# A decoder trunk on one core: fixing the order of VectorE and ScalarE from the second half of the output projection to the second classic pair

## The chip, the cores and the metric

The kernel runs on one core of one Trainium2 chip. The metric is the device time of one execution in microseconds (us); the time before is the median of three executions. In the profile PE is TensorE (matmuls), DVE is VectorE, ACT is ScalarE, POOL is GpSimd and SP is SyncE, which issues the DMAs. The program is one fixed list of instructions per engine; each engine works through its list in order and waits at an instruction whose inputs or buffers are not ready.

## What is computed

One layer with a sequence of 1024 tokens and a width of 1024, all in float32:

```python
h = _rmsnorm(x, norm1_g) * (1.0 + sc1) + sh1
z = h @ w_in
# forgetting attention on q, k, v and causal pooling on u give "mixed"
x = x + g1 * (mixed @ w_out)
h = _rmsnorm(x, norm2_g) * (1.0 + sc2) + sh2
a = h @ ffn_up                  # 1024 -> 2*2816
conv = conv_b + causal depthwise conv of width 3 of a
gate, val = split(conv, 2)
x = x + g2 * ((silu(gate) * val) @ ffn_down)
return _rmsnorm(x, final_g)
```

## The kernel before, in words

Every float32 product is made of three matmuls: an operand is split into a high part (a cast) and a low part (the operand minus its cast), and high by high, high by low and low by high are added in PSUM. So each operand of TensorE costs one cast, mostly on ACT, and one subtraction, mostly on DVE.

Around the change the work runs through these steps. Tokens come in eight tiles of 128 (t = 0 to 7).

- **Output projection, second half** (`wo_gen(1, t)`, then `wo_finish(1, t)`): TensorE fills the bank `po` of tile t; DVE multiplies by the gate (`ot`, L1129) and adds to the residual `x1[t]` (L1130); SP stores it (L1132). ACT squares and sums (L1135), ACT and DVE make the reciprocal root (L230, L231, L236 to L239, 128x1 each), DVE scales `xn` (L1137).
- **Transposition** (`make_h2T(t)`, called two steps later): TensorE transposes `xn` in eight 128x128 pieces (L1166), ACT evicts four of them (L1171) and DVE four (L1173) into `hn`, ACT casts the high part `HIb` (L1176), and the low part `LOb` is subtracted at L1178, on GpSimd for t below 6 and on DVE for t = 6 and 7. The transposes of tiles 6 and 7 stand inside the first classic banks.
- **Sums** (`tsums(t)`, t = 0 to 3): tiles t and t + 4 are combined on DVE (L1186, L1188, L1189, L1192) into three operands, and each is split (`put_quad`: ACT casts at L1153, DVE subtractions at L1155). They fill the `TQ` tiles 1, 2 and 3. Each TQ tile takes a quarter from each t, so it is whole after `tsums(3)`. `put_t4(t)` (L1197, L1198) puts the last of the sums back into `HIb` and `LOb`.
- **The MLP's up-projection.** Its columns come in 22 units of 128 gate and 128 value columns. Units 0 and 1 are "classic": four banks `uc` each (gate or value, first or second 512 tokens), 24 matmuls per bank (L1348 to L1350), copied out by ACT (L1353); `gate` and `value` then do the convolution (ACT L1361, DVE L1363 twice), Silu (ACT L1307, with a table load), the product (L1311) and its split. From unit 2 on a unit takes seven products of 12 matmuls (a Strassen scheme; banks `ua`, `ub`, `uc`) in the order 1, 5, 6, 2, 7, 3, 4. Product 1 reads `HIb` and `LOb`; product 5 reads TQ tile 1, product 6 TQ tile 2 and adds onto the bank of product 1, which ACT copies out first (L1323).
- **Weights of the units**: `load_x_up(j)` issues the loads of `wraw` on SP (L1238). `prep(j, p)` makes the left operand of a product: sums on DVE (L1268 to L1277) and a split by `hl` (ACT L1250, DVE L1251). From unit 2 on `wraw` lies in the same pool of nine buffers ("qk") as `x1` and `hn`, so a load waits until the last reader of an old `hn` is done.

TensorE's order is written out by hand for the whole program. For DVE and ACT a hand-written order (a `manual_schedule` block for the two engines in `ENG`) ends with the attention; from the output projection on the tile scheduler sets it, and it mixes the steps above.

Of the kernel before, what the change touches and what calls it, by code (L numbers as in the profile page):

```python
# [21 lines left out]
KT = D // 128  # L22
TT = S // 128
# [27 lines left out]
def kernel(  # L51
# [7 lines left out]
    nc = tc.nc  # L59
# [30 lines left out]
    def Tmx(name, shape=(128, 1024), dt=F32):  # L90
        return T("mx", list(shape), dt, name, 8)
# [885 lines left out]
    def wo_gen(dh, t):  # L977
        ts_ = slice(t * 128, (t + 1) * 128)
        po = pos[dh, t] = B1("po")
        for n, k in enumerate(KORD):  # L980
            while not (k in split_done and (dh, k) in wo):
                bg(1, 1, 1)
            h, l = wo[dh, k]
            mm(po, lhsT=HI[k][:, ts_], rhs=h, start=n == 0, stop=False)  # L984
            yield
            mm(po, lhsT=HI[k][:, ts_], rhs=l, start=False, stop=False)  # L986
            yield
            mm(po, lhsT=LO[k][:, ts_], rhs=h, start=False, stop=n == KT - 1)  # L988
            yield
# [130 lines left out]
    acth = dr.tile([NF, 128, S], F32, name="acth")  # L1120
    actl = dr.tile([NF, 128, S], F32, name="actl")

    def wo_finish(dh, t):
        ds_ = slice(dh * 512, (dh + 1) * 512)
        if dh == 0:
            x1.append(Tqk(f"x1{t}", (128, 1024), F32))
            nc.sync.dma_start(out=x1[t], in_=x[t * 128:(t + 1) * 128, :])
        tmp = Tpt("ot", (128, 512), F32)
        nc.vector.tensor_mul(out=tmp, in0=pos[dh, t], in1=g1b[:, ds_])  # L1129
        nc.vector.tensor_add(out=x1[t][:, ds_], in0=x1[t][:, ds_], in1=tmp)  # L1130
        if dh == 1:
            nc.sync.dma_start(out=x1d[t], in_=x1[t])  # L1132
            xn = Tp("xn")
            ss = Ts("ss2", 1)
            nc.scalar.activation(out=xn, in_=x1[t], func=AF.Square, accum_out=ss)  # L1135
            y = rstd_of(ss, "n2")
            nc.vector.tensor_scalar(out=xn, in0=x1[t], scalar1=y, scalar2=None, op0=ALU.mult)  # L1137
            hns[t] = xn

# [13 lines left out]
            nc.vector.tensor_sub(out=quad(n, 1, k)[:, :, cs], in0=s[:, 2 * k:2 * k + 2, :],  # L1155
                                 in1=f(quad(n, 0, k)[:, :, cs]))

    def make_h2T(t):
        ts_ = slice(t * 128, (t + 1) * 128)
        xn = hns[t]  # L1160
        hn = hn_[t] = Tqk("hn", (128, 1024), F32)
        for g in range(2):
            tp = B1("tp2")
            for q in range(4):
                j = g * 4 + q
                nc.tensor.transpose(tp[:, q * 128:(q + 1) * 128], xn[:, j * 128:(j + 1) * 128], ident)  # L1166
            for q in range(4):
                j = g * 4 + q
                o, i_ = hn[:, j * 128:(j + 1) * 128], tp[:, q * 128:(q + 1) * 128]
                if g == 0:  # L1170
                    nc.scalar.activation(out=o, in_=i_, func=AF.Identity, scale=A2[:, j:j + 1], bias=H2[:, j:j + 1])  # L1171
                else:
                    nc.vector.tensor_scalar(out=o, in0=i_, scalar1=A2[:, j:j + 1], scalar2=H2[:, j:j + 1],  # L1173
                                            op0=ALU.mult, op1=ALU.add)
        hv = hn.rearrange("p (a b) -> p a b", b=128)
        nc.scalar.copy(out=HIb[:, :, ts_], in_=hv)  # L1176
        eng = nc.gpsimd if t < 6 else nc.vector
        eng.tensor_sub(out=LOb[:, :, ts_], in0=hv, in1=f(HIb[:, :, ts_]))  # L1178

    def tsums(t):  # L1180

        cs = slice(t * 128, (t + 1) * 128)
        ha, hb = (hn_[a].rearrange("p (a b) -> p a b", b=128) for a in (t, t + 4))
        a1, a2, b1, b2 = ha[:, 0:4, :], ha[:, 4:8, :], hb[:, 0:4, :], hb[:, 4:8, :]
        V = nc.vector
        V.tensor_sub(out=a1, in0=b1, in1=a1)  # L1186
        put_quad(1, a1, cs)
        V.tensor_sub(out=b1, in0=b2, in1=b1)  # L1188
        V.tensor_sub(out=b2, in0=b2, in1=a1)  # L1189
        put_quad(2, b2, cs)  # L1190
        put_quad(3, b1, cs)
        V.tensor_sub(out=a2, in0=a2, in1=b2)  # L1192

    def put_t4(t):
        a2 = hn_[t].rearrange("p (a b) -> p a b", b=128)[:, 4:8, :]
        ts_ = slice(512 + t * 128, 640 + t * 128)
        nc.scalar.copy(out=HIb[:, 0:4, ts_], in_=a2)  # L1197
        nc.vector.tensor_sub(out=LOb[:, 0:4, ts_], in0=a2, in1=f(HIb[:, 0:4, ts_]))  # L1198

    for t in range(TT):  # L1200
# [4 lines left out]
    for t in range(TT):
        take(wo_gen(1, t), 99)
        wo_finish(1, t)
        if t >= 2:
            make_h2T(t - 2)

# [14 lines left out]
    def load_x_up(j):  # L1228
        for m in range(2):
            c0 = m * DFF + j * 128  # L1230
            if j == 0:
                hs = [Twr("wraw", (128, 4, 128)) if (m, k) != (1, 1) else
                      Tfb("wraw")[:, 0:512].rearrange("p (a b) -> p a b", b=128) for k in range(2)]
            else:
                r = (Tp if j == 1 else Tqk)("wraw", (128, 8, 128), F32)
                hs = [r[:, 0:4, :], r[:, 4:8, :]]
            for k in range(2):
                nc.sync.dma_start(out=hs[k], in_=ffn_up[k * 512:(k + 1) * 512, c0:c0 + 128]  # L1238
                                  .rearrange("(k p) c -> p k c", p=128))
                X[j, m, k] = hs[k]  # L1240
# [59 lines left out]
    def get(j, n, w=1024):  # L1300
        if (j, n) not in cpy:
            cpy[j, n] = (Tmx if j < NCL or n in ("p15", "u2") else Tqk)(n, (128, w), F32)
        return cpy[j, n]

    def gate(j):
        tg = cpy[j, "tg"] = conv(get(j, "cg"), j, "tg")
        nc.scalar.activation(out=tg, in_=tg, func=AF.Silu)  # L1307
# [31 lines left out]
    def classic(j, seq, after):

        done = {}
        for n, (m, ch) in enumerate(seq):
            b = B1("uc")
            sl = slice(ch * 512, (ch + 1) * 512)
            for k in range(KT):
                h, l = WT[j, (m, k // 4)]
                h, l = h[:, k % 4, :], l[:, k % 4, :]
                mm(b, lhsT=h, rhs=HI[k][:, sl], start=k == 0, stop=False)  # L1348
                mm(b, lhsT=h, rhs=LO[k][:, sl], start=False, stop=False)
                mm(b, lhsT=l, rhs=HI[k][:, sl], start=False, stop=k == KT - 1)  # L1350
                if j == 0 and (n, k) in ((0, 2), (1, 1)):
                    make_h2T(6 + n)
            nc.scalar.copy(out=get(j, "cv" if m else "cg")[:, sl], in_=b)  # L1353
            done[m] = done.get(m, 0) + 1
            if done[m] == 2:
                (value if m else gate)(j)
            after(n)
# [10 lines left out]
    for m in range(2):
        l2 = Tmx("ul0", (128, 8, 128), R)
        for k in range(2):  # L1370
            hl(0, (m, k), X[0, m, k], l2[:, 4 * k:4 * k + 4, :])
    load_x_up(1)
    for m in range(2):
        for k in range(2):
            hl(1, (m, k), X[1, m, k])

    def after0(n):
        if n:
            tsums(n - 1)

    def after1(n):
        if n == 0:
            tsums(3)
            load_x_up(2)
        if n == 1:
            for t in range(4):
                put_t4(t)

    classic(0, ((0, 0), (1, 0), (0, 1), (1, 1)), after0)
    classic(1, ((0, 1), (1, 1), (0, 0), (1, 0)), after1)  # L1390
# [239 lines left out]
```

## Time and profile before

| what | value |
|---|---|
| median of 3 executions | 1147.97 us (1146.52 to 1148.39) |
| the profiled execution: time, span | 1145.94 us, 1144.2 us |
| mean granted clock of TensorE in it | 0.976 of full speed |
| busy: PE, DVE, ACT, POOL | 1078.0, 882.3, 591.3, 199.3 us |
| chain that ended last, by engine | PE 55%, DVE 25%, DMA 8%, issue 5%, ACT 4% |

The profiled execution is 2.03 us shorter than the median. "Busy" counts time in which at least one instruction of the engine runs; the chain is followed back from the last instruction to whatever released each step. All times on the clock below count from the span's start: the second half of the output projection begins at about 413 us, the first classic bank at 458.71 and product 1 of unit 2 at 518.14.

### The profile page before, as it was taken

What the parts mean: (1) busy time and instruction counts of PE and PEld (TensorE: products, weight loads), DVE (VectorE), ACT (ScalarE), POOL (GpSimd) and SP (SyncE); (2) the same over time, 40 slices, a digit from 0 to 9 for tenths busy, and PEclk for the clock granted to TensorE, in tenths of its full rate; (3) what the DMA queues carried; (4) which work ended last, traced back from release to release, by engine and by line L of the source; (5) the groups of instructions that cost most, each with busy time, mean ns of one, the idle gap of its engine ahead of it and who ended that gap; (6) DMA issues with size and microseconds to landing.
All of it is one profiled execution on the core that took longest, in us unless ns stands there. A gap on an engine that the chain in (4) does not pass through costs nothing.

```text
span 1144.2 us, 15550 instructions
## 1 busy us (share of the span) xinstructions
PE 1078.0 (94%) x5382; PEld 896.8 (78%) x5382; DVE 882.3 (77%) x1559; ACT 591.3 (52%) x1074; POOL 199.3 (17%) x191
## 2 busy tenths in 40 slices
PE   7899999989999999699999999999999589999996
PEld 7679887778877888588888888887877468788885
DVE  6987588787677647977787878878788549958986
ACT  7663445545577325665454545555555325524444
POOL 4564243354366303100000000000000000000000
PEclk9799999999999999899999999999999889999998
DMA  9963256452425211222424242534433399983475
GB/s 294 279 189 76 61 190 184 125 136 47 70 63 183 96 43 69 93 93 74 145 77 144 77 140 81 165 112 137 139 112 128 119 366 386 334 263 104 138 244 207
DMA packets 143143, 171.10 MB, mean 150 GB/s; under 512 B 10125, under 2 KB 94937, under 8 KB 143065
## 3 DMA queue, kind: packets, MB, share of 16 engines
q1 hardware_dynamic: 143065, 170.11, 47.0%
q8 instruction: 42, 0.69, 0.3%
q14 instruction: 36, 0.29, 0.1%
HBM read 128.62 MB, written 37.27 MB: 145 GB/s over the span
## 4 chain that ended last, share of the span: by engine, by line
PE 55%; DVE 25%; DMA 8%; issue 5%; ACT 4%; SPq 2%; POOL 0%; DVEq 0%; ACTq 0%; POOLq 0%
PE ua L1285 13%; PE ub L1285 7%; PE z L923 5%; PE db L1285 5%; PE da L1285 4%; DVE accd L308 3%; PE uc L1285 3%; DMA wraw<-in_ffn_up_dram 3%; DMA mrow<-in_mod_w_dram 2%; PE pv L829 2%; PE po L986 2%; PE po L988 2%; DVE tg L1363 2%; PE po L984 2%; PE tpp L806 1%
## 5 line engine op out<-in xcount | busy, mean ns | idle before, releaser
L1250 ACT CAST uh<-wraw 128x512 fp32r<-128x512 f32 x128 | 73.2, 619 | 111.7 <-DVE wraw L1270 64.4
L1285 PE MATMUL ua<-t,uh 128*128 128x512 f32 x320 | 99.4, 392 | 2.5 <-ACT u L1327 2.4
L1251 DVE TENSOR_TENSOR ul<-wraw,uh 128x512 fp32r<-128x512 f32 x128 | 87.4, 684 | 8.8 <-PE po L986 4.0
L793 POOL TENSOR_SCALAR P<-P,ri 128x128 f32<-128x128 f32 (+3 forms) x64 | 65.6, 1026 | 136.5 <-DVE ri L792 127.9
L786 ACT ACTIVATE P<-P,mn 128x128 f32<-128x128 f32 (+3 forms) x64 | 49.7, 777 | 75.7 <-DVE mn L775 41.5
L1285 PE MATMUL da<-th,sh 128*128 128x512 f32 x176 | 70.0, 398 | 15.9 <-ACT th L1486 15.9
L810 DVE TENSOR_TENSOR pl<-tpp,ph 128x512 fp32r<-128x512 f32 (+1 forms) x80 | 50.7, 634 | 34.1 <-ACT ph L809 33.8
L1285 PEld LDWEIGHTS ua<-t,uh 128*128 128x128 f32 x320 | 59.6, 188 | 17.2 <-ACT u L1327 5.1
L1285 PE MATMUL da<-th,sl 128*128 128x512 f32 x176 | 69.7, 396 | 2.3 <-DVE sl L1491 2.3
L1285 PE MATMUL da<-tl,sh 128*128 128x512 f32 x176 | 69.7, 396 | 0.0
L775 DVE CUSTOM_DVE_ANT_0 P<-s,Fb 128x512 f32<-128x512 f32 (+2 forms) x96 | 50.2, 551 | 16.7 <-PE s L773 7.0
L1285 PE MATMUL ua<-t,ul 128*128 128x512 f32 x160 | 62.3, 389 | 0.0
L1285 PE MATMUL ua<-HIb,uh 128*128 128x512 f32 x160 | 62.2, 389 | 0.0
L1285 PE MATMUL ua<-LOb,uh 128*128 128x512 f32 x160 | 62.2, 389 | 0.0
L1285 PE MATMUL ua<-HIb,ul 128*128 128x512 f32 x160 | 62.2, 389 | 0.0
L923 PE MATMUL z<-HIb,wh 128*128 128x512 f32 x144 | 59.9, 416 | 0.0
L1363 DVE SCALAR_TENSOR_TENSOR tg<-cg,colB,tg 128x1023 f32<-128x1023 f32 (+1 forms) x44 | 56.3, 1279 | 4.5 <-ACT tg L1361 3.5
L923 PE MATMUL z<-LOb,wh 128*128 128x512 f32 x144 | 58.7, 408 | 0.0
L923 PE MATMUL z<-HIb,wl 128*128 128x512 f32 x144 | 58.5, 406 | 0.0
L1363 DVE SCALAR_TENSOR_TENSOR tvv<-cv,colB,tvv 128x1023 f32<-128x1023 f32 (+1 forms) x44 | 56.2, 1277 | 0.1
L809 ACT CAST ph<-tpp 128x512 fp32r<-128x512 f32 (+1 forms) x80 | 43.1, 540 | 19.5 <-PE tpp L802 9.8
L1285 PEld LDWEIGHTS da<-th,sh 128*128 128x128 f32 x176 | 33.7, 192 | 23.5 <-ACT th L1486 16.4
(310 smaller groups left out, 3179.1 us busy)
## 6 DMA issues: line engine op xcount, KB each, us to landing
wraw<-in_ffn_up_dram SPq DMA_DIRECT2D x88, 256.0 KB, 4.6
mrow<-in_mod_w_dram SPq DMA_DIRECT2D x32, 512.0 KB, 8.2
actd<-tvv SPq DMA_DIRECT2D x22, 512.0 KB, 2.7
ra<-in_ffn_down_dram SPq DMA_DIRECT2D x44, 256.0 KB, 4.3
sh<-acth SPq DMA_DIRECT2D x33, 256.0 KB, 4.1
sl<-actl SPq DMA_DIRECT2D x33, 256.0 KB, 4.4
x<-in_x_dram SPq DMA_DIRECT2D x16, 512.0 KB, 5.1
mst<-in_mod_w_dram SPq DMA_DIRECT2D x32, 256.0 KB, 5.4
```

Source lines behind the costliest of these rows:

```text
L308: nc.vector.scalar_tensor_tensor(out=acc, in0=m, scalar=cact[:, k, 1:2], in1=acc, op0=ALU.mult, op1=ALU.add)
L775: nc.vector.tensor_tensor_reduce(out=pt[:, n0:n1], in0=s[:, 0:n], in1=Fb[:, n0:n1], scale=1.0, scalar=3.0e38, op0=ALU.add, op1=ALU.min, ac ...
L786: nc.scalar.activation(out=pt, in_=pt, func=AF.Exp, scale=-1.0, bias=mn, accum_out=rs)
L793: nc.gpsimd.tensor_scalar(out=pt, in0=pt, scalar1=ri, scalar2=1.0, op0=ALU.mult, op1=ALU.mult)
L809: nc.scalar.copy(out=ph[:, 0:W], in_=tp[:, 0:W])
L810: nc.vector.tensor_sub(out=pl[:, 0:W], in0=tp[:, 0:W], in1=f(ph[:, 0:W]))
L829: mm(o, lhsT=V, rhs=x_[:, sl], start=b == 0 and not lo, stop=bool(lo and diag and kb == 1))
L923: mm(t[ch], lhsT=w[:, k, :], rhs=act[kk][:, ch * 512:(ch + 1) * 512], start=i == 0 and m == 0 and p0, stop=i == 1 and m == 3 and p1)
L1250: nc.scalar.copy(out=h, in_=src)
L1251: nc.vector.tensor_sub(out=l, in0=src, in1=f(h))
L1285: mm(*a, skip_group_check=True, **k)
L1363: nc.vector.scalar_tensor_tensor(out=t[:, sh:S], in0=s[:, 0:S - sh], scalar=cw_col[w][:, jj:jj + 1], in1=t[:, sh:S], op0=ALU.mult, op1=ALU ...
```

## The change

`wo_finish` and `make_h2T` are cut into pieces (`fin_a`, `fin_sq`, `fin_xn`; `tr`, `ev`, `hi2`, `lo2`), `classic` into `cl_mm` and `cl_ev`, and the calls are written out in one order inside a `manual_schedule` block for DVE and ACT. ACT now evicts five transposed pieces and DVE three; the subtraction of `LOb` runs on DVE for every tile, so six instructions of GpSimd go. The splits of unit 0's weights stand inside the steps of t = 4 to 7, those of unit 1 further back; their loads are issued earlier. Bank (unit 1, gate, first half) moves to the third place. The diff, cut:

```diff
-    def make_h2T(t):
...
+    def ev(t):
+        hn = hn_[t] = Tqk("hn", (128, 1024), F32)
+        for j in range(8):
...
+            if j < 5:
+                nc.scalar.activation(out=o, in_=i_, func=AF.Identity, scale=A2[:, j:j + 1], bias=H2[:, j:j + 1])
+            else:
+                nc.vector.tensor_scalar(out=o, in0=i_, scalar1=A2[:, j:j + 1], scalar2=H2[:, j:j + 1],
+                                        op0=ALU.mult, op1=ALU.add)
...
-        eng = nc.gpsimd if t < 6 else nc.vector
-        eng.tensor_sub(out=LOb[:, :, ts_], in0=hv, in1=f(HIb[:, :, ts_]))
...
+    def lo2(t):
+        ts_ = slice(t * 128, (t + 1) * 128)
+        nc.vector.tensor_sub(out=LOb[:, :, ts_], in0=hn_[t].rearrange("p (a b) -> p a b", b=128),
+                             in1=f(HIb[:, :, ts_]))
...
+    trans = ExitStack()
+    trans.enter_context(tc.manual_schedule(engines=ENG))
     load_x_up(0)
...
     load_x_up(1)
...
+    for t in range(TT):
+        take(wo_gen(1, t), 99)
+        if t >= 2:
+            tr(t - 2)
+        fin_a(1, t)
+        if t >= 3:
+            ev(t - 3)
+        fin_sq(t)
+        if t >= 3:
+            hi2(t - 3)
+        if t >= 4:
...
+            hl_cl(0, m, k, l0[m][:, 4 * k:4 * k + 4, :])
+        fin_xn(t)
+        if t >= 3:
+            lo2(t - 3)
+    cl_mm(0, 0, 0, {1: 6, 6: 7})
+    ev(5)
+    hi2(5)
+    lo2(5)
+    hl_cl(1, 0, 0)
+    cl_mm(0, 1, 0)
+    ev(6)
+    cl_ev(0, 0, 0)
+    hi2(6)
+    hl_cl(1, 0, 1)
+    ev(7)
+    lo2(6)
+    hi2(7)
+    lo2(7)
+    cl_mm(1, 0, 0)
+    cl_ev(0, 1, 0)
+    tsums(0)
+    cl_mm(0, 0, 1)
+    cl_ev(1, 0, 0)
+    tsums(1)
+    cl_mm(0, 1, 1)
+    cl_ev(0, 0, 1)
+    hl_cl(1, 1, 0)
+    hl_cl(1, 1, 1)
+    gate(0)
+    cl_mm(1, 0, 1)
+    cl_ev(0, 1, 1)
+    tsums(2)
+    load_x_up(2)
+    value(0)
+    cl_mm(1, 1, 1)
+    cl_ev(1, 0, 1)
+    tsums(3)
+    cl_mm(1, 1, 0)
+    cl_ev(1, 1, 1)
+    trans.close()
+    for t in range(4):
+        put_t4(t)
+    gate(1)
+    cl_ev(1, 1, 0)
+    value(1)
```

What this does to the engines' lists is seen best in the lists. In the changed file the lines lie further down: Square is L1137, `xn` L1142, the DVE eviction L1178, the `LOb` subtraction L1186, the sums L1195 to L1201 with their splits at L1157 (ACT) and L1159 (DVE), `put_t4` L1206 and L1207, `hl` L1253 and L1254, `prep` L1271 to L1280, Silu L1310, the copy of product 1 L1326.

First place: DVE in the projection's step t = 5 (`x_4776` is `x1[5]`), as a difference of the two lists.

```order
-L1173 TENSOR_SCALAR hn<-tp_5196,A_915,H_916 128x128 x4
-L230 TENSOR_SCALAR n2a<-ss_5174 128x1
+L1178 TENSOR_SCALAR hn<-tp_5116,A_915,H_916 128x128 x3
+L230 TENSOR_SCALAR n2a<-ss_5202 128x1
+L1254 TENSOR_TENSOR ul_5142<-wraw,uh 128x512
 L236 RECIPROCAL n2y<-n2y 128x1
 L237 TENSOR_TENSOR n2t<-n2y 128x1
 L238 SCALAR_TENSOR_TENSOR n2t<-n2t,n2a 128x1
 L239 SCALAR_TENSOR_TENSOR n2y<-n2t,n2y 128x1
-L1137 TENSOR_SCALAR xn<-x_4776,n2y 128x1024
+L1142 TENSOR_SCALAR xn<-x_4776,n2y 128x1024
+L1186 TENSOR_TENSOR LOb<-hn,HIb 128x8x128
```

One eviction leaves the step; a split of a weight (`ul`) comes in ahead of the reciprocal, and the `LOb` subtraction behind `xn`.

Second place: DVE at the last sums, `tsums(3)`, in the list before (`t_5478` and `t_5480` are the low halves of TQ tile 1, `t_5496` and `t_5498` those of TQ tile 3).

```order
L1186 TENSOR_TENSOR hn<-hn 128x512
L1192 TENSOR_TENSOR hn<-hn 128x512
L1155 TENSOR_TENSOR t_5488<-hn,t_5484 128x2x128
L1155 TENSOR_TENSOR t_5490<-hn,t_5486 128x2x128
L1178 TENSOR_TENSOR LOb<-hn,HIb 128x8x128
L1155 TENSOR_TENSOR t_5478<-hn,t_5474 128x2x128
L1155 TENSOR_TENSOR t_5480<-hn,t_5476 128x2x128
L1188 TENSOR_TENSOR hn<-hn 128x512
L1155 TENSOR_TENSOR t_5496<-hn,t_5492 128x2x128
L1155 TENSOR_TENSOR t_5498<-hn,t_5494 128x2x128
```

And DVE from `tsums(2)` to `tsums(3)` in the list of the change (`t_5497` and `t_5499` are now the low halves of TQ tile 1; `s_5897` is the weight sum of unit 3).

```order
L1198 TENSOR_TENSOR hn<-hn 128x512
L1271 TENSOR_TENSOR s_5897<-wraw 128x512
L1254 TENSOR_TENSOR ul<-wraw,uh 128x512
L1272 TENSOR_TENSOR wraw<-wraw 128x512
L1159 TENSOR_TENSOR t_5507<-hn,t_5503 128x2x128
L1159 TENSOR_TENSOR t_5509<-hn,t_5505 128x2x128
L1159 TENSOR_TENSOR t_5515<-hn,t_5511 128x2x128
L1159 TENSOR_TENSOR t_5517<-hn,t_5513 128x2x128
L1201 TENSOR_TENSOR hn<-hn 128x512
L1254 TENSOR_TENSOR ul<-wraw,uh 128x512
L1363 SCALAR_TENSOR_TENSOR tvv<-cv,colB,tvv 128x1023
L1280 TENSOR_TENSOR wraw<-wraw 128x512
```

Before, TQ tile 1 was finished ahead of the classic units' convolutions and of every preparation of unit 2. Now the scheduler, which still places what is outside the block, has put the preparations of units 2 and 3 between the sums, and the convolutions of unit 0 stand ahead of `tsums(3)`.

Third place: ACT around `tsums(3)` in the list of the change (`p_5793` takes the bank of product 1 of unit 2).

```order
L1357 COPY cg<-uc 128x512
L1361 ACTIVATE tg<-cg,colB 128x1024
L1157 CAST t_5493<-hn 128x2x128
L1157 CAST t_5495<-hn 128x2x128
L1310 ACTIVATE tg<-tg 128x1024
L1157 CAST t_5503<-hn 128x2x128
L1157 CAST t_5505<-hn 128x2x128
L1157 CAST t_5511<-hn 128x2x128
L1157 CAST t_5513<-hn 128x2x128
L1357 COPY cv<-uc 128x512
L1326 COPY p_5793<-ua 128x512
```

Before, the copy of product 1 stood behind the convolution and Silu of unit 1 alone; all casts of the sums came earlier. Now the casts of `tsums(3)` and the Silu of unit 1 stand ahead of it.

## Rows read from the trace of the kernel before

**Rows 1.** The page, part 1: busy time, share and instructions of each engine.

```profile
PE 1078.0 (94%) x5382; PEld 896.8 (78%) x5382; DVE 882.3 (77%) x1559; ACT 591.3 (52%) x1074; POOL 199.3 (17%) x191
```

**Rows 2.** Waits, PE, 380 to 530 us: in total, times, longest.

```profile
PE tp L1166 <- DVE xn L1137: 9.9, 2, 6.8
```

**Rows 3.** Windows: length, busy (count) per engine, PE's clock, DMA, GB/s.

```profile
464.10:471.60 7.50, 7.49 (x29) 5.83 (x29) 7.50 (x17) 5.68 (x14) 2.41 (x1) 0.77 0.58 182
471.60:478.40 6.80, 0.01 (x1) 0.00 (x0) 6.80 (x17) 3.21 (x7) 0.00 (x0) 0.80 0.12 33
478.40:485.00 6.60, 6.58 (x25) 5.64 (x26) 6.60 (x15) 3.88 (x9) 0.00 (x0) 0.69 0.29 82
485.00:518.10 33.10, 33.10 (x147) 27.27 (x146) 24.37 (x38) 19.42 (x33) 0.00 (x0) 1.00 0.26 80
```

**Rows 4.** Timeline of PE: start, length, instruction, [idle before, releaser].

```profile
426.25 1.03 PE L1166 MATMUL tp<-ident,xn 128*128 128x128 f32 x8
...
432.58 1.03 PE L1166 MATMUL tp<-ident,xn 128*128 128x128 f32 x8
...
458.71 0.48 PE L1348 MATMUL uc<-HIb,uh 128*128 128x512 f32 x1
...
518.14 0.39 PE L1285 MATMUL ua<-HIb,uh 128*128 128x512 f32 x1
...
520.86 0.62 PE L1285 MATMUL ub<-t,uh 128*128 128x512 f32 x2
...
523.58 0.62 PE L1285 MATMUL ua<-t,uh 128*128 128x512 f32 x2
```

**Rows 5.** Timeline of POOL.

```profile
437.86 2.38 POOL L1178 TENSOR_TENSOR LOb<-hn,HIb 128x1024 fp32r<-128x1024 f32 x1 [5.02 <-ACT HIb L1176]
```

**Rows 6.** Timeline of DVE: one small operation without and beside POOL's work.

```profile
424.53 0.16 DVE L237 TENSOR_TENSOR n2t<-n2y 128x1 f32<-128x1 f32 x1
...
438.27 1.98 DVE L237 TENSOR_TENSOR n2t<-n2y 128x1 f32<-128x1 f32 x1
```

**Rows 7.** Lines by form, DVE, 415 to 520 us: busy, mean ns, idle before.

```profile
L1173 DVE TENSOR_SCALAR hn<-tp,A,H 128x128 f32<-128x128 f32 x32 | 10.9, 401 | 0.0
L237 DVE TENSOR_TENSOR n2t<-n2y 128x1 f32<-128x1 f32 x8 | 10.7, 1334 | 0.3
L1155 DVE TENSOR_TENSOR t<-hn,t 128x256 fp32r<-128x256 f32 x24 | 9.0, 416 | 0.0
...
L1363 DVE SCALAR_TENSOR_TENSOR tg<-cg,colB,tg 128x1023 f32<-128x1023 f32 x2 | 2.6, 1280 | 1.5 <-ACT tg L1361 1.5
...
L1178 DVE TENSOR_TENSOR LOb<-hn,HIb 128x1024 fp32r<-128x1024 f32 x2 | 2.4, 1215 | 0.0
```

**Rows 8.** Timeline of DVE: a step's start, the last splits of TQ tile 1, a load.

```profile
421.32 0.69 DVE L1129 TENSOR_TENSOR ot<-po,g1b 128x512 f32<-128x512 f32 x1
...
485.38 0.76 DVE L1155 TENSOR_TENSOR t<-hn,t 128x256 fp32r<-128x256 f32 x2
...
496.02 0.69 DVE L1268 TENSOR_TENSOR s<-wraw 128x512 f32<-128x512 f32 x1 [2.31 <-DMA wraw<-in_ffn_up_dram]
```

**Rows 9.** Timeline of ACT: the same step, casts, a table load, a copy.

```profile
422.83 1.06 ACT L1135 ACTIVATE xn<-x 128x1024 f32<-128x1024 f32 x1 [2.99 <-DVE x L1130]
...
424.01 0.29 ACT L231 ACTIVATE n2y<-ss,cact 128x1 f32<-128x1 f32 x1
...
429.31 1.05 ACT L1176 CAST HIb<-hn 128x1024 fp32r<-128x1024 f32 x1
...
470.92 0.62 ACT L1250 CAST uh<-wraw 128x512 fp32r<-128x512 f32 x1
...
498.76 1.28 ACT L1307 ACT_TABLE_LOAD   x1
...
521.94 0.58 ACT L1323 COPY p<-ua 128x512 f32<-128x512 f32 x1
```

**Rows 10.** The page, part 6: one DMA issue, KB, median us to landing.

```profile
wraw<-in_ffn_up_dram SPq DMA_DIRECT2D x88, 256.0 KB, 4.6
```

More of the change, by code (lines that the diff above doesn't have):

```diff
@@ L1121, with fin_a @@
     actl = dr.tile([NF, 128, S], F32, name="actl")
-    def wo_finish(dh, t):
+    def fin_a(dh, t):
         ds_ = slice(dh * 512, (dh + 1) * 512)
@@ L1132, in wo_finish, with fin_sq, fin_xn @@
             nc.sync.dma_start(out=x1d[t], in_=x1[t])
[L1133 to L1138, printed above, removed]
+    def fin_sq(t):
+        hns[t] = Tp("xn")
+        ss = Ts("ss2", 1)
+        nc.scalar.activation(out=hns[t], in_=x1[t], func=AF.Square, accum_out=ss)
+        rs[t] = rstd_a(ss, "n2")
+    def fin_xn(t):
+        y = rstd_b(*rs[t], "n2")
+        nc.vector.tensor_scalar(out=hns[t], in0=x1[t], scalar1=y, scalar2=None, op0=ALU.mult)
     TQ = {}
@@ L1156, in put_quad, with tr, hi2 @@
                                  in1=f(quad(n, 0, k)[:, :, cs]))
-    def make_h2T(t):
-        ts_ = slice(t * 128, (t + 1) * 128)
-        xn = hns[t]
-        hn = hn_[t] = Tqk("hn", (128, 1024), F32)
+    tps = {}
+    def tr(t):
         for g in range(2):
-            tp = B1("tp2")
+            tp = tps[t, g] = B1("tp2")
             for q in range(4):
                 j = g * 4 + q
[L1166 to L1176, printed above, removed]
-        eng = nc.gpsimd if t < 6 else nc.vector
-        eng.tensor_sub(out=LOb[:, :, ts_], in0=hv, in1=f(HIb[:, :, ts_]))
+                nc.tensor.transpose(tp[:, q * 128:(q + 1) * 128], hns[t][:, j * 128:(j + 1) * 128], ident)
+    def ev(t):
+        hn = hn_[t] = Tqk("hn", (128, 1024), F32)
+        for j in range(8):
+            o, i_ = hn[:, j * 128:(j + 1) * 128], tps[t, j // 4][:, (j % 4) * 128:(j % 4 + 1) * 128]
+            if j < 5:
[3 more added lines that the diff above has]
+                                        op0=ALU.mult, op1=ALU.add)
+    def hi2(t):
+        nc.scalar.copy(out=HIb[:, :, t * 128:(t + 1) * 128], in_=hn_[t].rearrange("p (a b) -> p a b", b=128))
+    def lo2(t):
+        ts_ = slice(t * 128, (t + 1) * 128)
+        nc.vector.tensor_sub(out=LOb[:, :, ts_], in0=hn_[t].rearrange("p (a b) -> p a b", b=128),
+                             in1=f(HIb[:, :, ts_]))
     def tsums(t):
@@ L1201 @@
         take(wog[t] if t < 4 else wo_gen(0, t), 99)
-        wo_finish(0, t)
+        fin_a(0, t)
         if t >= 4:
             load_wo(1, t - 4, Tmx if t < 7 else Tv)
[L1205 to L1209, printed above, removed]
     lo_, hi_ = slice(0, 512), slice(512, 1024)
@@ L1337, in post, with cl_mm, cl_ev @@
             value(j)
[L1339 to L1357, printed above, removed]
+    def cl_mm(j, m, ch, mid=None):
+        b = banks[j, m, ch] = B1("uc")
+        sl = slice(ch * 512, (ch + 1) * 512)
+        for k in range(KT):
+            h, l = WT[j, (m, k // 4)]
+            h, l = h[:, k % 4, :], l[:, k % 4, :]
+            mm(b, lhsT=h, rhs=HI[k][:, sl], start=k == 0, stop=False)
+            mm(b, lhsT=h, rhs=LO[k][:, sl], start=False, stop=False)
+            mm(b, lhsT=l, rhs=HI[k][:, sl], start=False, stop=k == KT - 1)
+            if mid and k in mid:
+                tr(mid[k])
+    def cl_ev(j, m, ch):
+        sl = slice(ch * 512, (ch + 1) * 512)
+        nc.scalar.copy(out=get(j, "cv" if m else "cg")[:, sl], in_=banks[j, m, ch])
     def conv(s, jj, name):
@@ L1365, in conv, with hl_cl @@
         return t
+    def hl_cl(j, m, k, l=None):
+        hl(j, (m, k), X[j, m, k], l)
+    trans = ExitStack()
+    trans.enter_context(tc.manual_schedule(engines=ENG))
     load_x_up(0)
[L1368 to L1371, printed above, removed]
     load_x_up(1)
[L1373 to L1390, printed above, removed]
+    l0 = {}
+    rs = {}
+    for t in range(TT):
[9 more added lines that the diff above has]
+        if t >= 4:
+            m, k = divmod(t - 4, 2)
+            if k == 0:
+                l0[m] = Tmx("ul0", (128, 8, 128), R)
+            hl_cl(0, m, k, l0[m][:, 4 * k:4 * k + 4, :])
[43 more added lines that the diff above has]
+    value(1)
     UORD = (1, 5, 6, 2, 7, 3, 4)
```

## Prediction

> **What bounds the kernel now.** I read the page first: TensorE is busy for 94% of the span [rows 1], so time can be gained where it waits or runs slowly and lost where a new wait begins. The waits of TensorE between 380 and 530 us come next: only the transposes of tiles 6 and 7 wait, for `xn`, 9.9 us in two waits, the longer 6.8 [rows 2]. The windows show what a wait costs beyond itself: in the 7.5 us behind the first one the granted clock was 0.77, in the 6.6 us behind the second 0.69, and from 485 on 1.00 [rows 3]. Lost to the slow clock are (1 - 0.77) x 7.5 = 1.7 and (1 - 0.69) x 6.6 = 2.0 us. With no wait at all 9.9 + 3.7 = **13.6 us** would come back; that is the ceiling of any gain here.
>
> Why `xn` is late stands in the same windows: DVE is busy for all of 464.1 to 485 [rows 3]. It has two loads. One is GpSimd: its `LOb` subtraction ends at 437.86 + 2.38 = 440.24, and a 128x1 operation of DVE beside it, 0.16 us elsewhere, takes 1.98 and ends at 440.25 [rows 5, 6]. The other is the sums, which stand between the steps. They are early, though: TQ tile 1 is whole at 486.1 [rows 8], long before product 5 reads it at 520.86 [rows 4].
>
> **The change, part by part.** *GpSimd goes.* Eight of those small operations took 10.7 us where 8 x 0.16 = 1.3 would do, so 9.4 us of DVE come free; six subtractions of 1.215 us, 7.3 in all, come on top [rows 6, 7]. DVE's net work falls by 2.1 us. The Trainium skill, "Perfetto Trace Analysis", section "Optimizing Scalar/DVE Operations", says that with a saturated DVE it may make sense to give work to ScalarE or even GpSimd. By that alone the change would be wrong by the 7.3 us; by the rows it is right by 2.1.
>
> *The projection's steps.* In the new order everything of a step hangs on one chain from ot: 1.51 us to Square, 1.18 to the root [rows 8, 9]; then on ACT root, `HIb` cast and `uh`, 0.29 + 1.05 + 0.62 [rows 9], some 1.75 with their overlaps; then on DVE the split (0.69 like any 128x512 operation [rows 8]), four small operations 0.2 apart, `xn` (I take 0.75; bounds are 0.69 for half its width and 1.215 for `LOb` [rows 7, 8]) and `LOb`, 1.2. Together 1.51 + 1.18 + 1.75 + 0.69 + 0.78 + 0.75 + 1.2 = 7.9, less overlaps 7.7. TensorE's step is 432.58 - 426.25 = 6.33 [rows 4]. So steps 4 to 7 start at 439.0 (TensorE's time), 446.7, 454.4 and 462.1 and end at 469.8. `LOb` of tile 3, which the first classic bank needs at its second matmul, is ready at 462.1 instead of early: TensorE waits 3.4 us from 458.71 on [rows 4], plus 1.7 for the clock as behind the 3-us wait above. The transposes of tiles 6 and 7 find `xn` at about 461 and 469 and wait little. From there eight banks and product 1 run at 33.1 / 147 = 0.225 per matmul [rows 3]: 462.1 + 1.7 + 192 x 0.227 + 16 transposes at 0.1 = 509.0. I add 0.9 for one short wait on tile 7's `LOb`, so product 1 starts at **509.9 instead of 518.14** [rows 4], 8.2 us earlier.
>
> *Tiles 5 to 7.* Behind 469.8 DVE has nine evictions, three `LOb` and two `ul`: 9 x 0.32 + 3 x 1.13 + 2 x 0.6 = 7.5 us, each 0.08 under its mean as operations overlap [rows 7, 8]. It alternates with ACT tile by tile (fifteen evictions, three casts, two `uh`, one copy), and following both lists row by row I get four waits of 0.6 to 1.7 us, 4.8 together. So the sums begin only at 482.1 to 482.6.
>
> *The sums.* One `tsums` costs DVE four operations of 0.6 and six of 0.34, 4.4 us [rows 7, 8], plus two waits of 0.6 in which ACT casts, since each split now stands directly behind the subtraction that feeds it: 5.7. `tsums(0)` ends at 488.3. Inside `tsums(1)` now stands the preparation of unit 2, two operations (1.2), and its load can only be issued when `tsums(0)` has released a buffer: 488.4 + 4.6 to 5.0 [rows 10] = 493.2, where DVE has stood since about 491.5. The trace of before has such a wait, 2.31 us [rows 8]. `tsums(1)` ends near 496.5. Five 128x512 operations and two of 1.28 [rows 7] follow: 502. In `tsums(2)` the scheduler has put two subtractions of `put_t4` ahead of the splits; their casts on ACT stand behind a table load of 1.28 [rows 9], Silu (about 1.1) and a copy, and the Silu waits for DVE's `tg`, ready at 502.2: DVE waits some 2.9 us, to 505.6. The first of these frees the buffer of unit 3's load: issued 506.4, landed 511.2, DVE waiting 2.4 for it. `tsums(2)` ends at 515.0, the convolution of unit 0 and four further small groups at 522.6, with another wait of 0.7 for a cast. `tsums(3)` has one operation of 1.28 in it and a wait of 0.5, and its first splits come out at 524.2 (ACT's half) and **525.5** (DVE's half).
>
> *Products 5 and 6 of unit 2.* Product 1 ends at 509.9 + 2.7 = 512.6. Product 5 then waits for TQ tile 1 until 524.1, 11.5 us, and 1.35 more for the low half. The clock falls as it does behind the old 6.8-us wait, another 2.0. Product 6 adds onto the bank of product 1, which ACT copies out behind Silu, four casts and a copy, 1.1 + 1.3 + 0.5 + 0.6 from 527.6 on: 531.1, instead of 523.58 [rows 4]. Before, that copy ran at 521.94 [rows 9].
>
> **Sum:** 531.1 - 523.58 = **+7.5 us**. Nothing behind product 6 gives it back: TensorE was busy from there on in the trace of before, and the steps behind hang on TensorE. Against the profiled execution that is 1145.94 + 7.5 = 1153.4; against the median, 2.03 higher, 1155.5. I take 1154.5 between them. Bounds: if both loads have landed in time, 3.6 us go: +3.9. If the loads take twice as long, 4 to 5 us come on top of either: +12.
>
> **Rivals.** *A, faster: the queue keeps up.* From 469.8 to 525.5 are 55.7 us, of which 14.8 are DVE's waits by the working above; 40.9 are work. Without waits TQ tile 1 would be whole at 510.7, before product 1 ends, and the gain of 8.2 us would stand: 1147.97 - 8.2 = 1139.8. The point from which it decides: DVE waits less than 2 us in that stretch. For it speaks that DVE was hardly ever idle between 464 and 485 [rows 3] while the scheduler mixed the steps; against it that the new list puts each reader directly behind its source. The Trainium skill, "SBUF — State Buffer", section "Who interferes with whom", holds that GpSimd and the second port of DVE exclude each other; the trace agrees (1.98 against 0.16 us), and if more operations of DVE than the eight were slowed so, this is the rival that it helps. Chance 0.11.
>
> *B, no change: the scheduler's insertions cost nothing.* Both loads land in time and the `put_t4` subtractions don't wait: 7.5 - 3.6 - 2.9 = +1.0, so 1147 to 1150. For it: SP and the DMA queues are little used here (share 0.26 [rows 3]). Against it: a load of before already came 2.31 us late [rows 8]. Chance 0.09.
>
> *C, slower still.* The backlog lasts: the casts and splits of products 2 and 7 stand behind the convolution of unit 1 as well, and each holds TensorE once more for a few microseconds: +11, 1158 to 1161. For it: at 531 DVE still has all of unit 1's value half ahead. Chance 0.12. That the block is left out of the built program is excluded by the lists shown.
>
> **How the numbers follow.** Forecast 0.68, A 0.11, B 0.09, C 0.12. A measurement of this kernel can tell about 0.2% from no change, 2.3 us, so the bounds lie at 1145.7 and 1150.3. Faster is A; same is B; slower is the forecast and C: 0.11, 0.09, 0.80. The forecast's own range is 1150.5 to 1158; the range reaches down into B and up into C, 1148.5 to 1160.5, and leaves out A, the lower half of B and little else, somewhat under 0.2.
>
> **What would show it.** In the profile after: `n2t` at 0.16 us in every step; projection steps of DVE 7.7 apart; a TensorE wait of 3 to 4 us for `LOb` in the first `uc` bank instead of the waits for `xn`; product 1 of unit 2 near 510; then one wait of about 12 us of `ub` for `t`, and product 6 at 531. DVE's idle time between 470 and 525 should be near 15 us, with two waits on `wraw` loads. It is wrong if `ub` starts before 516, if the wait of `ub` is under 5 us, or if TensorE makes up time behind 531.

## The result and the profile after

The changed kernel took 1153.22 us (median of five, 1149.45 to 1156.5) against 1147.97 before (median of five by now, 1144.2 to 1148.68): 1.0058 times, 95% interval 1.0041 to 1.0075. It is slower by 4.7 to 8.6 us. The ratio is estimated from all executions of both kernels; the two medians alone would give 1.0046, and the ratios further down differ from those of their medians by up to 0.0014. All are to the kernel before, measured on the same chip; runs 1 to 4 below are of one chip, runs 5 to 8 of another, so runs of the two groups are compared by their ratios.

The profiled execution (1152.65 us) shows where. First its page, part 1, to set against [rows 1]:

```profile
span 1150.9 us, 15529 instructions
...
PE 1078.1 (94%) x5382; PEld 894.6 (78%) x5382; DVE 879.5 (76%) x1557; ACT 593.3 (52%) x1082; POOL 182.9 (16%) x185
```

No engine has much more to do: ACT, which evicts one piece more per tile, is busy 2.0 us longer, TensorE as long as before, DVE even 2.8 us less, though it took over six subtractions, and GpSimd 16.4 us less. So the time lies in waits. Those of TensorE from 400 to 600 us, after:

```profile
PE ub L1288 <- ACT t L1157: 9.5, 1, 9.5
PE uc L1350 <- DVE LOb L1186: 2.9, 1, 2.9
PE ua L1288 <- ACT p L1326: 0.6, 1, 0.6
PE ub L1288 <- DVE t L1159: 0.6, 1, 0.6
```

The 9.9 us for `xn` [rows 2] are gone. In their place stand 2.9 us for `LOb` in the first classic bank, 9.5 and 0.6 of product 5 for the two halves of `t`, TQ tile 1, and 0.6 of product 6 for `p`, together 13.6. TensorE's timeline at the places of [rows 4]:

```profile
429.25 1.03 PE L1169 MATMUL tp<-ident,xn 128*128 128x128 f32 x8
...
461.71 0.48 PE L1349 MATMUL uc<-HIb,uh 128*128 128x512 f32 x1
465.06 0.50 PE L1350 MATMUL uc<-LOb,uh 128*128 128x512 f32 x1 [2.87 <-DVE LOb L1186]
...
512.16 0.39 PE L1288 MATMUL ua<-HIb,uh 128*128 128x512 f32 x1
...
524.50 0.80 PE L1288 MATMUL ub<-t,uh 128*128 128x512 f32 x1 [9.46 <-ACT t L1157]
525.86 0.80 PE L1288 MATMUL ub<-t,uh 128*128 128x512 f32 x1 [0.56 <-DVE t L1159]
...
531.32 0.73 PE L1288 MATMUL ua<-t,uh 128*128 128x512 f32 x2 [0.59 <-ACT p L1326]
```

The first transposes start 3.00 us later than before (429.25 against 426.25), and TensorE has 2402 matmuls ahead of that point in both. In runs 4 and 5 below, which share the changed kernel's order up to there, they start at 424.98 and 424.80, earlier than before. So this part of the difference is not the change's. I therefore measure from these transposes to the first matmul of product 6 and call it **the stretch**: 523.58 - 426.25 = 97.33 us before, 531.32 - 429.25 = 102.07 after, **4.74 more**. Within it the gain was there first: product 1 starts 82.91 us into the stretch instead of 91.89, 9.0 earlier. Then product 5 waits, and 13.7 us are lost between product 1 and product 6. The slow clock takes its part, as the windows around the waits show (columns as in [rows 3]):

```profile
465.00:469.00 4.00, 3.94 (x14) 3.39 (x15) 2.41 (x7) 2.60 (x5) 0.00 (x0) 0.57 0.33 131
469.00:514.90 45.90, 45.90 (x206) 37.55 (x205) 34.03 (x64) 28.27 (x58) 0.00 (x0) 1.00 0.17 47
...
524.50:531.30 6.80, 5.67 (x12) 3.76 (x12) 5.92 (x11) 3.52 (x9) 0.00 (x0) 0.57 0.12 44
```

Product 5 takes 531.32 - 524.50 = 6.82 us from its first matmul to product 6; before, it took 2.72 [rows 4]. Of the 4.1 us between, 0.56 and 0.59 are the two short waits, and the other 2.95 go with the granted clock, 0.57 of full speed in this window, behind a wait of 9.46. So the 13.7 us are 9.46 + 0.56 + 0.59 of waits, 10.6 together, and about 3 of slow clock.

Why `t` is late is on DVE's timeline: two steps of the projection, the start of the sums, and the waits in them.

```profile
449.72 0.69 DVE L1129 TENSOR_TENSOR ot<-po,g1b 128x512 f32<-128x512 f32 x1
...
454.13 0.69 DVE L1254 TENSOR_TENSOR ul<-wraw,uh 128x512 fp32r<-128x512 f32 x1 [1.63 <-ACT uh L1253]
...
457.32 0.68 DVE L1129 TENSOR_TENSOR ot<-po,g1b 128x512 f32<-128x512 f32 x1
...
484.87 0.68 DVE L1195 TENSOR_TENSOR hn<-hn 128x512 f32<-128x512 f32 x1
...
495.00 0.69 DVE L1271 TENSOR_TENSOR s<-wraw 128x512 f32<-128x512 f32 x1 [1.15 <-DMA wraw<-in_ffn_up_dram]
...
507.21 1.29 DVE L1207 TENSOR_TENSOR LOb<-hn,HIb 128x512 fp32r<-128x512 f32 x2 [2.85 <-ACT HIb L1206]
...
511.84 0.69 DVE L1271 TENSOR_TENSOR s<-wraw 128x512 f32<-128x512 f32 x1 [1.34 <-DMA wraw<-in_ffn_up_dram]
...
525.38 0.75 DVE L1159 TENSOR_TENSOR t<-hn,t 128x256 fp32r<-128x256 f32 x2
```

A step takes 457.32 - 449.72 = 7.60 us, with 1.63 of waiting for ACT's `uh` in it; the sums run from 484.87 until TQ tile 1 is whole at 526.1, 40 us later on this clock than before [rows 8]. Of the 55.7 us from 472.8 to 528.5 DVE is idle for 12.6.

### The profile page after: what moved, and what is told of

Read it like the earlier page. It is cut to its first block, busy times and chain, and to the rows that moved or that the text cites. A ratio compares the mean times of both kernels' runs of the same rounds, so it can differ in the third digit from the quotient of the medians.

```text
span 1150.9 us, 15529 instructions
## 1 busy us (share of the span) xinstructions
PE 1078.1 (94%) x5382; PEld 894.6 (78%) x5382; DVE 879.5 (76%) x1557; ACT 593.3 (52%) x1082; POOL 182.9 (16%) x185
## 4 chain that ended last, share of the span: by engine, by line
PE 53%; DVE 23%; DMA 9%; ACT 5%; issue 5%; SPq 4%; POOL 0%; DVEq 0%; ACTq 0%; POOLq 0%
PE ua L1288 11%; PE db L1288 7%; PE da L1288 7%; PE ub L1288 5%; PE z L923 5%; DMA wraw<-in_ffn_up_dram 4%; DMA mrow<-in_mod_w_dram 3%; PE uc L1288 3%; DVE tg L1363 2%; DVE accd L308 2%; DVE tvv L1363 2%; PE po L984 2%; PE po L986 2%; PE po L988 2%; PE pv L829 2%
## 5 line engine op out<-in xcount | busy, mean ns | idle before, releaser
L1253 ACT CAST uh<-wraw 128x512 fp32r<-128x512 f32 x128 | 72.9, 619 | 98.7 <-DVE wraw L1273 53.1
L1254 DVE TENSOR_TENSOR ul<-wraw,uh 128x512 fp32r<-128x512 f32 x128 | 87.3, 684 | 9.0 <-ACT uh L1253 8.5
L1288 PE MATMUL da<-th,sh 128*128 128x512 f32 x176 | 69.5, 395 | 15.7 <-ACT th L1530 15.3
L1288 PE MATMUL ub<-t,uh 128*128 128x512 f32 x160 | 51.6, 403 | 10.0 <-ACT t L1157 9.5
```

What stands on the lines that cost most here:

```text
L1288: mm(*a, skip_group_check=True, **k)
```

## The experiments

The theory: the hand-written order puts the last sums, and ACT's copy of product 1's bank, behind work that TensorE doesn't need yet. Rivals: the subtractions that came to DVE are the cause; or the projection's slower steps are. The last column counts from the first transposes as well, but to the first matmul of product 2, which follows product 6: in runs 4, 5 and 8 waits or the slow clock fall into product 6 itself, behind the end of the stretch.

| kernel | ratio (95% interval) | stretch, us | to product 2, us |
|---|---|---|---|
| kernel before | 1 | 97.33 | 100.05 |
| changed kernel | 1.0058 (1.0041 to 1.0075) | 102.07 | 104.91 |
| 1: LOb on GpSimd again | 1.0095 (1.008 to 1.011) | 105.16 | 108.04 |
| 2: kernel before, LOb on DVE | 0.9957 (0.9942 to 0.9973) | 92.03 | 94.75 |
| 3: splits early | 1.0008 (0.9987 to 1.0028) | 96.56 | 99.42 |
| 4: sums first | 1.0064 (1.0039 to 1.0089) | 99.73 | 104.65 |
| 5: 4 with the fixed part ended behind the sums | 0.9956 (0.994 to 0.9973) | 90.14 | 94.42 |
| 6: fixed part ended ahead of the sums | 0.9994 (0.998 to 1.0009) | 95.35 | 98.07 |
| 7: 3 and 6 | 0.9962 (0.9944 to 0.9979) | 90.86 | 93.58 |
| 8: 3 and 5 | 0.992 (0.9895 to 0.9945) | 84.75 | 90.59 |

The new share of the evictions and the moved bank are in the changed kernel and in every run but 2, and were not tried alone.

**1. LOb on GpSimd again.** The changed kernel with one part undone:

```diff
     def lo2(t):
         ts_ = slice(t * 128, (t + 1) * 128)
-        nc.vector.tensor_sub(out=LOb[:, :, ts_], in0=hn_[t].rearrange("p (a b) -> p a b", b=128),
+        eng = nc.gpsimd if t < 6 else nc.vector
+        eng.tensor_sub(out=LOb[:, :, ts_], in0=hn_[t].rearrange("p (a b) -> p a b", b=128),
```

> The changed kernel with one part undone: the LOb subtraction of tiles 0 to 5 is on GpSimd again. By the theory (the fixed order puts the last sums behind the convolution of unit 0, and TensorE waits for TQ tile 1) nothing essential changes: product 5 still waits 9 to 12 us for t. Each of the later projection steps loses 1.13 us of LOb on DVE and gets some 1.9 us back through an operation held beside GpSimd, so the step grows from 7.6 to 8.0 to 8.4 us; the time is 1.004 to 1.010 of before. By the first rival (the subtractions that came to DVE, 7.3 us, are what made it late) the wait of product 5 shrinks by 5 to 7 us and the time returns to 0.998 to 1.002 of before.

It is slower still, 1.0095, as the theory expected; product 5 waits 9.3 us for `t`. GpSimd's and DVE's timelines in a step:

```profile
453.45 2.39 POOL L1187 TENSOR_TENSOR LOb<-hn,HIb 128x1024 fp32r<-128x1024 f32 x1 [5.85 <-ACT HIb L1182]
```

```profile
449.51 0.68 DVE L1129 TENSOR_TENSOR ot<-po,g1b 128x512 f32<-128x512 f32 x1
...
453.93 2.46 DVE L1255 TENSOR_TENSOR ul<-wraw,uh 128x512 fp32r<-128x512 f32 x1 [1.64 <-ACT uh L1254]
...
457.75 0.68 DVE L1129 TENSOR_TENSOR ot<-po,g1b 128x512 f32<-128x512 f32 x1
```

Now it is the weight split that runs beside GpSimd, 2.46 us instead of 0.69, and the step grows to 8.24 us. Giving the subtractions back to GpSimd gave no time back. By itself that doesn't refute the first rival, since a step's DVE work did not fall: 1.22 us went and 1.77 came. What refutes the rival are runs 2 and 5 to 8: there all eight subtractions are on DVE, and product 5 waits for nothing.

**2. The kernel before with LOb on DVE**, this part alone:

```diff
-        eng = nc.gpsimd if t < 6 else nc.vector
-        eng.tensor_sub(out=LOb[:, :, ts_], in0=hv, in1=f(HIb[:, :, ts_]))
+        nc.vector.tensor_sub(out=LOb[:, :, ts_], in0=hv, in1=f(HIb[:, :, ts_]))
```

> The kernel before with one part of the change alone: the LOb subtraction on DVE for all eight tiles, the order left to the scheduler. Theory: this part is a gain, since the small operations held beside GpSimd (about 2 us each) cost more than the subtractions add; the longer of the waits for xn goes or shrinks to 2 us, the one for tile 6 may grow, and the time is 0.994 to 0.997 of before. First rival (7.3 us more on DVE delay xn): both waits grow, 1.003 to 1.008 of before.

0.9957, a gain of some 5 us from one line. As expected, the wait of tile 7 is gone and that of tile 6 grew, from 3.1 to 5.3 us; DVE's steps come every 6.3 us instead of 7.4. TensorE's waits between 400 and 600 us are down from 9.9 to

```profile
PE tp L1166 <- DVE xn L1137: 5.3, 1, 5.3
```

So one part of the change is a gain by itself, and what the changed kernel loses comes from the rest of it: the order, the places of the splits and the share of the evictions.

**3. Splits early.** The changed kernel with the four splits of unit 0's weights ahead of the steps:

```diff
+    for m in range(2):
+        l0[m] = Tmx("ul0", (128, 8, 128), R)
+        for k in range(2):
+            hl_cl(0, m, k, l0[m][:, 4 * k:4 * k + 4, :])
     for t in range(TT):
...
-        if t >= 4:
...
-            hl_cl(0, m, k, l0[m][:, 4 * k:4 * k + 4, :])
```

> The changed kernel with the four splits of unit 0's weights ahead of the projection's steps instead of inside steps 4 to 7. Both theories expect DVE's steps to come down from 7.6 us to TensorE's 6.33, the wait of the first classic bank for LOb (2.9 us) to go and product 1 to start some 5 us earlier than in the changed kernel. The theory of the order: the sums move forward with it, product 5 still waits 9 to 12 us behind product 1, and the stretch from the first transposes to product 6 is 97 to 99 us (before 97.3, changed 102.1): 0.998 to 1.003 of before. The second rival (the slow steps are the cause): the wait of product 5 is under 5 us and the time is 0.990 to 0.995.

1.0008, as the theory of the order has it (the stretch, 96.56, is just below its 97 to 99). DVE's steps are down to 6.33 us. The wait for `LOb` is gone and product 1 starts earlier, but product 5 waits as long as ever behind it; the waits from 400 to 600 us:

```profile
PE ub L1288 <- ACT t L1157: 9.0, 1, 9.0
PE ua L1288 <- ACT p L1326: 1.0, 1, 1.0
PE ub L1288 <- DVE t L1159: 0.6, 1, 0.6
```

The slow steps cost 102.07 - 96.56 = 5.5 us of the stretch, but the wait of product 5 isn't theirs.

**4. Sums first.** The changed kernel with the last two sums ahead of unit 0's gate and value:

```diff
     hl_cl(1, 1, 1)
-    gate(0)
+    tsums(2)
     cl_mm(1, 0, 1)
     cl_ev(0, 1, 1)
-    tsums(2)
+    tsums(3)
     load_x_up(2)
+    gate(0)
     value(0)
     cl_mm(1, 1, 1)
     cl_ev(1, 0, 1)
-    tsums(3)
     cl_mm(1, 1, 0)
```

> The changed kernel with the sums of tiles 2 and 3 ahead of the gate and value of unit 0 in the fixed order. If the late TQ tile 1 alone holds TensorE, product 5 starts at once and the time is 0.990 to 0.996 of before. My theory says that the wait moves: the whole fixed order, with unit 0's convolution at its end, still stands ahead of ACT's copy of product 1's bank, so product 5 starts without a wait but product 6 waits 11 to 14 us for that copy (p), and the time is 1.003 to 1.009 of before, about that of the changed kernel.

1.0064, as expected. Product 5 doesn't wait any more; product 6 does, in the waits from 400 to 600 us:

```profile
PE ua L1288 <- ACT p L1326: 11.2, 1, 11.2
PE uc L1350 <- DVE LOb L1186: 2.9, 1, 2.9
```

ACT's timeline shows what the copy of product 1's bank stands behind:

```profile
515.17 1.28 ACT L1310 ACT_TABLE_LOAD   x1 [1.21 <-DVE tg L1363]
516.47 1.06 ACT L1310 ACTIVATE tg<-tg 128x1024 f32<-128x1024 f32 x1
517.43 1.22 ACT L1361 ACTIVATE tvv<-cv,colB 128x1024 f32<-128x1024 f32 x1
522.58 0.62 ACT L1318 CAST ah<-tvv 128x512 fp32r<-128x512 f32 x1 [3.93 <-DVE tvv L1314]
523.11 0.58 ACT L1357 COPY cg<-uc 128x512 f32<-128x512 f32 x1
523.58 0.59 ACT L1357 COPY cv<-uc 128x512 f32<-128x512 f32 x1
524.06 0.60 ACT L1326 COPY p<-ua 128x512 f32<-128x512 f32 x1
```

Product 1 had ended before 510.60, where product 5 starts in this run. The copy, 0.60 us of work, ran at 524.06, behind unit 0's Silu and convolution; the longest of ACT's waits there is the 3.93 us at `ah` in which DVE finished unit 0's value. Neither engine was busy throughout TensorE's wait:

```profile
513.30:524.70 11.40, 0.19 (x1) 0.00 (x0) 6.88 (x7) 6.21 (x9) 0.00 (x0) 0.60 0.12 46
```

Of these 11.40 us DVE was busy for 6.88 and ACT for 6.21: they waited for each other inside a piece that TensorE didn't need.

**5. Sums first, the fixed part ended behind them.** One line of 4 moved: the block of fixed order ends behind `tsums(3)`.

```diff
     tsums(3)
+    trans.close()
     load_x_up(2)
     gate(0)
...
-    trans.close()
```

> The order of the run with the sums first, with the fixed part ending behind the last sums, so that the gate and value of unit 0 and ACT's copies are left to the scheduler. Theory: the copy of product 1 is no longer behind unit 0's convolution; the 11-us wait for p shrinks to 2 to 4 us, and the time is 0.996 to 1.001 of before, against 1.006 for the same order with the longer fixed part. If something else than the fixed list held that copy, the wait stays above 8 us and the time above 1.003.

0.9956 against 1.0064 for 4: 11 to 12 us by this line, slightly more than expected. The wait for `p`, put at 2 to 4 us, is gone altogether:

```profile
PE uc L1350 <- DVE LOb L1186: 2.9, 1, 2.9
PE ua L1288 <- ACT t L1157: 1.6, 1, 1.6
PE ua L1288 <- DVE t L1159: 1.1, 1, 1.1
```

**6. The fixed part ended ahead of the sums.** The changed kernel with `trans.close()` behind `lo2(7)`.

```diff
     lo2(7)
+    trans.close()
     cl_mm(1, 0, 0)
...
-    trans.close()
```

> The changed kernel with the fixed order ending behind the LOb subtraction of tile 7: steps and tiles 5 to 7 stay fixed, everything from the sums on is left to the scheduler. Theory: the waits of product 5 for t and of product 6 for p go altogether, since no hand-written list stands between; what stays is the slow steps with the splits (first classic bank waits 3 to 4 us for LOb) and one or two short waits of later classic banks; 0.997 to 1.002 of before. If the steps or the LOb subtractions were the cause, product 5 would still wait 5 us or more and the time be 1.004 or above.

0.9994, not to be told from before, as expected. Products 5 and 6 wait for nothing; what is left, but for 0.4 us at a transposition, are classic banks that wait for `LOb`, a cast and a split:

```profile
PE uc L1350 <- DVE LOb L1186: 5.1, 2, 3.5
PE uc L1349 <- ACT uh L1253: 1.3, 1, 1.3
PE uc L1351 <- DVE ul L1254: 0.9, 1, 0.9
```

**7. Edits 3 and 6 together.**

> The splits of unit 0's weights ahead of the steps, and only steps and tiles 5 to 7 fixed, the sums left to the scheduler. Theory: steps of 6.33 us and no wait for xn in the transposes, as the fixed order was able to give, and no wait of products 5 and 6; some 3 to 5 us of short waits of classic banks for weights and LOb remain: 0.992 to 0.997 of before. If the fixed sums and not the steps were where the fixed order helps, it is at 1.000 or above.

0.9962, as expected. Waits of 4.8 us remain between 400 and 600 us, all in classic banks, and none for `xn`.

**8. Edits 3 and 5 together:** splits early, sums first, the fixed part ended behind them.

> Three edits together on the changed kernel: the splits of unit 0's weights ahead of the steps, the sums of tiles 2 and 3 ahead of gate and value, the fixed part ending behind the sums. Theory: no wait for LOb in the first classic bank, product 1 about 5 us earlier than in the changed kernel, products 5 and 6 held 2 to 5 us together: 0.991 to 0.995 of before, 1137 to 1142 us, at or below the 1140.6 of the kernel before with LOb on DVE alone. If fixing an order costs here in any form, it stays above 0.996.

0.992, 1137.52 us, as expected: faster than both kernels. Against 2 the intervals just overlap (0.9945 and 0.9942), so that it beats 2 as well is likely and not certain. TensorE's waits from 400 to 600 us are down to two, both in product 6:

```profile
510.84 0.51 PE L1288 MATMUL ua<-t,uh 128*128 128x512 f32 x1 [1.28 <-ACT t L1157]
512.47 0.50 PE L1288 MATMUL ua<-t,uh 128*128 128x512 f32 x1 [1.13 <-DVE t L1159]
...
516.68 0.39 PE L1288 MATMUL uc<-HIb,uh 128*128 128x512 f32 x1
```

ACT copies product 1's bank 0.2 us after product 5 has started (506.67), having waited for TensorE alone:

```profile
506.87 0.59 ACT L1326 COPY p<-ua 128x512 f32<-128x512 f32 x1 [1.92 <-PE ua L1288]
```

Its stretch, 84.75 us, is 12.6 below that of before, near the 13.6 that the prediction gave as the ceiling, but its time is only 9 to 10 us lower. The difference lies in product 6, which takes 516.68 - 510.84 = 5.84 us here, with the wait of 1.13 and a granted clock of 0.78 (510.8 to 514.8) and 0.84 (514.8 to 520) in it. Before, it took 526.30 - 523.58 = 2.72:

```profile
526.30 0.39 PE L1285 MATMUL uc<-HIb,uh 128*128 128x512 f32 x1
```

Up to product 2 the gain is 100.05 - 90.59 = 9.46 us, and from there to the end both profiles take 617.9. With an earlier TQ tile 2 some 3 us more might come back, by this difference; that was not tried.

## Why the prediction was right, and where its sizes were off

The forecast was slower by the wait of product 5, 1154.5 us in a range of 1148.5 to 1160.5; it came to 1153.22. The mechanism was the one forecast: all named waits but one (0.9 us on tile 7's `LOb`) came where they were put, and none of the stated signs of being wrong did. Step by step, with 3.0 us taken off the clock readings of after, by which its stretch began later:

- *GpSimd goes*: the eight `n2t` take 1.3 us instead of 10.7 [rows 7], and the eight `LOb` subtractions 1.22 each, as taken. Runs 1 and 2 show the sign of the net term in both orders: 3.1 and 5.3 us of the stretch. The 2.1 us by which the prediction let DVE's work fall were too few: the trace of before has one more operation held beside GpSimd, a sum at L1192 (line below), 2.02 us instead of 0.68. That makes 3.4; that the rest is DVE standing on the path at single steps, where each such delay comes out whole, is my reading and not tried. First the line from DVE's timeline before, then the groups that give the two prices, from the lines by form of after, DVE, 415 to 530 us:

```profile
469.65 2.02 DVE L1192 TENSOR_TENSOR hn<-hn 128x512 f32<-128x512 f32 x1
```

```profile
L1186 DVE TENSOR_TENSOR LOb<-hn,HIb 128x1024 fp32r<-128x1024 f32 x8 | 9.8, 1220 | 1.2 <-ACT HIb L1182 1.2
...
L237 DVE TENSOR_TENSOR n2t<-n2y 128x1 f32<-128x1 f32 x8 | 1.3, 160 | 0.3
```

- *Projection steps*: 7.60 us against 7.7. The step that starts at 457.32 was put at 454.4 and came at 454.3. First bank: a wait of 2.87 against 3.4.
- *Product 1*: 509.2 against 509.9. The wait on tile 7's `LOb` (0.9) did not come.
- *The sums begin* at 481.9 against 482.1 to 482.6.
- *The wait behind Silu's table load*, 2.85 against 2.9. The two waits on loads came where they were said to, but took 1.15 and 1.34 against 1.7 (493.2 - 491.5) and 2.4. This is the term that was mis-sized: I took 4.6 to 5.0 us to landing [rows 10]. The trace gives the landing for two of the six loads of this stretch, 2.99 and 3.41 us, and at the pair issued at 491.06 and 491.49 DVE's wait ended at 495.00, 3.5 us behind the second.
- *The lower bound.* The prediction takes 3.6 us off if both loads are in time; its own two waits are 4.1 together. So its lower bound should have been +3.4 and not +3.9, and rival B's sum +0.5 and not +1.0.
- *DVE's idle time* in the 55.7 us was 12.6 us against near 15.
- *Product 5* starts at 521.5 against 524.1 and waited 9.46 against 11.5; *product 6* starts at 528.3 against 531.1. The stretch is 4.7 longer instead of 7.5. The loads make 1.6 of the 2.8 between; the rest are tenths at the steps and tiles. The slow clock behind the wait cost 2.95 us where 2.0 was taken, and the copy of product 1 held product 6 for 0.59 where the sum has some 0.9 (524.1 + 1.35 + 2.72 + 2.0 = 530.2, then 531.1).
- *Behind product 6* next to nothing comes back: 1150.9 - 531.32 = 619.6 us against 620.6, one us less.

So the profiled difference of 6.7 us is 3.0 ahead of the stretch, 4.7 in it and 1.0 back behind it. That the profiled execution, 1152.65, comes within a microsecond of the 1153.4 forecast for it is luck: the 3.0 us ahead, which are not the change's, nearly make up for the 2.8 us that the stretch was put too long. Added to the median before, the stretch's 4.7 give 1152.7, and the forecast's 7.5 would have given 1155.5; the 1154.5 that I took between two readings was nearer by that choice.

The rivals: A (the queue keeps up) failed at its stated point: DVE idled 12.6 us and not under 2. Its condition was also too narrow. Run 8 has the whole gain that A spoke of, and runs 2, 5 and 7 a good part of it, by other lists than the changed kernel's, and DVE still idles 8.1 us in run 8 in the 55.7 us that lie as far behind the first transposes. What decided was where the idle time stood. B (the insertions cost nothing) failed: the `put_t4` wait came in full. C (the backlog lasts) did not show: behind the start of product 6 TensorE's waits are those of before within a few tenths, 15.3 against 15.9 us for `th` and 2.3 against 2.4 for `u`, and one of 0.5 is new.

What the prediction didn't see is what run 4 shows. I named the late sums as the cause and the copy behind them as a small extra of 1 us; with the sums early the copy alone costs 11.2 us. Both hang on the same length of fixed list, so moving the sums alone, as in run 4, helps nothing.

## What to carry to other kernels

In this kernel a hand-written order on two engines that feed each other paid only as far as it held what the next consumer needs. Where the fixed part goes on into later work, something outside it (in run 4 the copy of a finished bank, 0.6 us long) can queue behind that work and hold TensorE, there for 11 us. So end it where the last urgent result is written, put the urgent results first, and leave the rest to the scheduler: the same list, re-sorted, with its splits moved ahead and cut in this way, went from 1.0058 to 0.992. When a change does two things, run each alone: here the one was worth 5 us and the other cost more. And measure up to a point behind the last wait that the change can cause: a stretch that ended at product 6's first matmul showed run 8 as 3 us better than it is.

## What the runs showed that I had not expected

- Which operation of DVE suffers beside GpSimd's `LOb` depends on what comes at that moment. In the kernel before it is the 128x1 product `n2t` in five tiles (about 2.0 us instead of 0.16 [rows 6]) and once a 128x512 sum (2.02 instead of 0.68), in run 1 the 128x512 weight split in five tiles (2.42 to 2.48 instead of 0.69). All of these read two operands in SBUF, and none ended before GpSimd did. The reciprocals (0.16) and evictions (0.39 to 0.40) beside it in the kernel before took their usual time.
- Two loads of 256 KB whose landing the trace of after gives, a pair issued by itself, landed in 2.99 and 3.41 us. The four that the trace of before gives in this stretch, the last two of a group of four and the last two of a group of six, took 4.5 to 5.5. That the crowding is the reason was not tried.
- The time ahead of the stretch varies between executions: the first transposes started between 424.37 and 429.86 us in the ten profiles. A spread of 5.5 us is as large as what was to be measured, so a single time of this kernel can't show a change of that size, and the stretch within one profile tells more.
